# Two-layer hybrid backbone kernel: the second layer's output weights rounded in its half 0 and kept in DRAM, Fourier tables loaded one piece ahead, two splits and one stage put elsewhere in the order

## The chip, the cores and the metric

The kernel runs on one core of a Trainium2 chip. The core has TensorE (PE, matrix products), VectorE (DVE), ScalarE (ACT), GpSimd (POOL) and SyncE (SP), whose queue issues nearly all of this kernel's DMAs, one behind the other; 16 DMA engines carry them. The metric is the time of one execution in device microseconds, less is better. Times below are of single executions taken by the hardware profiler, or medians of timed runs where the text says so.

## The reference

Two layers over 2048 tokens and 256 context tokens of width 1024. A layer normalises, multiplies by one input matrix of 2816 columns, runs three groups of heads, gates them, multiplies by one output matrix, normalises again and adds.

```python
hx = rmsnorm(x, g_pre) * (1 + scale[:, None]) + shift[:, None]
q, k, v, ga, uf, gf, zc, bc, cc, gc = split_cols(hx @ w_in, PROJ_SIZES)
a = window_attention(rope(q), rope(k), v, kc, vc, sink_b)   # 128-token blocks, 256 context keys + 3 blocks
f = fourier_mix(uf, w_fourier)       # 2-D FFT as products with tables, real part, group product
s = short_conv_mix(zc, bc, cc, conv_w, conv_b)
h = concat([a * silu(ga), f * silu(gf), s * silu(gc)])
y = h @ w_out
x_new = x + gate[:, None] * rmsnorm(y, g_post)
```

The first layer also updates the context tokens; the second needs only their keys and values.

## The kernel before

**Precision.** Each fp32 operand is rounded to a high part in fp32r and a low part that holds the rest; a product is three products (hi·hi, hi·lo, lo·hi). The helper `split` makes the two parts: its first letter names the engine of the high part (L79 on DVE, L81 on ACT, L83 on POOL), the second that of the subtraction that gives the low part (L85 on DVE, L87 on POOL).

**Stages.** Each layer has phase 1, in two halves of 1024 tokens (half 0 also takes the context), and phase 2. Phase 1 projects: for each 128-column piece of the input weights (`wr` loaded on SP's queue at L124, split into `wh` and `wl`, two buffers each) `proj` runs eight k-steps of three products, L313, L314 and L315, into `acc`. Behind each k-step `tick()` advances the generators that are registered as fills: modulation, table splits, the FFT stages. In half 1 the fill `ffts` runs the two Fourier transforms: `fft_a`, then `fft_b`, which loads table pieces `ftb` from the DRAM copy `ftd` (L555, three buffers), forms `pf`, splits it into `PQ` and multiplies `PQ` by `AB` into `pm_` (L428 in both). `tab_gen` makes that copy in half 0 of layer 0: a piece `tr` is loaded, split into `th` (ACT and DVE), and stored. `form_b_w` loads the value-and-Fourier weights in four pieces and splits each into `wbh` (DVE) and `wbl`; it runs next to the key weights' piece.

In the profiled execution layer 0 has half 0 until about 345 us, half 1 until about 618 and phase 2 until about 1100; layer 1 half 0 until about 1335, half 1 until about 1604 and phase 2 until the end.

**Phase 2** goes over blocks of 128 tokens, two steps a block (one for each key head). In step s, `u_qk` (A) forms scores `sp` and their exponentials `pt`; `u_pv` (B) transposes them (`tp`), splits them into `ph` and `pl` and multiplies by the values into `op`; `u_out` (C) multiplies by the output weights into `yp` and finishes the block. Strings of letters, one letter a piece, say how the pieces follow each other. In the first steps C's place is taken by three late projections (`late`, through `lt`), and the letters V and W advance `wout_gen`, which makes one half of the output weights each: four loads of 512 KB (`wr<-in_wout`), each split straight into two resident tiles `big`. Phase 2 opens its first loads while phase 1 still runs.

**What sets the order.** The order on an engine is that of the program's text, with a scheduler that places what is ready; `behind(x)` keeps an instruction behind the named one. SP's queue is strictly in order: an issue that waits for a buffer holds everything behind it. `self.last_v` is the DVE instruction of the last split that used DVE; `self.last_st` is the last store of a gate.

```python
                load_wcf()
                wb = self.pool(wbs, f"wb{l}{half}", bufs=1)
                fetch(J_K)
                WB = self.form_b_w(l, wb)
```

Of the kernel before, what the change touches and what calls it, by code (L numbers as in the profile page):

```python
# [8 lines left out]
F32 = mybir.dt.float32  # L9
BF16 = mybir.dt.bfloat16  # L10
F32R = mybir.dt.float32r
# [5 lines left out]
DEPTH = 2  # L17
# [4 lines left out]
KT = 8  # L22
HALF = 1024
CH = 512
# [7 lines left out]
WE_A = ["vv", "av", "vv", "av"]  # L32
WE_B = ["vv", "vp", "vv", "av"]
WV_A = ["vv", "av", "vv", "vv"]
WV_B = ["vv", "av", "vv", "av"]
# [3 lines left out]
ORDER_3A = "bAAWCCBcBCABBAWCBBCBBCcACBCBB"  # L39
ORDER_3B = "bAAWCCBcBCABBAWCBBCBBCcACBCBB"  # L40
# [8 lines left out]
RT = 0.6, 0.594, 0.616, 0.1, 0.15, 0.12, 0.49, 0.16  # L49
# [11 lines left out]
def f(t):  # L61
    return t.bitcast(F32)


class Kern:
# [477 lines left out]
    def fft_b(self, fp, ps, AB, ct):  # L543
# [42 lines left out]
        for _ in range(4):  # L586
            yield
# [24 lines left out]
    def tab_gen(self, p):  # L612
        nc = self.nc
        for k in range(9):
            raw = p.tile([128, 384], F32, name="tr", tag="tr")
            nc.sync.dma_start(raw, self.I["ftab"][:, k])
            yield
            h = p.tile([128, 2, 384], F32R, name="th", tag="th")
            self.split(h[:, 0], h[:, 1], raw, "a", "v")
            nc.sync.dma_start(self.ftd[k], f(h))  # L620
            yield
# [160 lines left out]
    def half(self, l, half, ps, sv, tail):  # L782
# [4 lines left out]
        with ExitStack() as es:  # L787
# [119 lines left out]
            else:  # L907
# [16 lines left out]
                WB = self.form_b_w(l, wb)  # L924
# [47 lines left out]
            if l == 0 and half == 0:  # L972
                mp = self.pool(e3, "mp", bufs=1)
                fills.append(self.start_fill(self.tab_gen(mp), RT[5]))
            for ct in range(2):
# [181 lines left out]
    def u_pv(self, l, p, ps, B, kv):  # L1157
# [28 lines left out]
        for t in range(nkt):  # L1186
            if t + 1 < nkt:
                trans(t + 1)
                yield
            vv = B.vts[t][:, kv * 128:(kv + 1) * 128]  # L1190
            end = t == nkt - 1
            nc.tensor.matmul(op, vv, hl[t][0], start=(t == 0), stop=False)  # L1192
            nc.tensor.matmul(op, vv, hl[t][1], start=False, stop=end)  # L1193
            if kv == 1 and t == 1:
                B.hf = (p.tile([128, 4, 128], F32R, name="hfh", tag="hfh", bufs=1),
                        p.tile([128, 4, 128], F32R, name="hfl", tag="hfl", bufs=1))
                self.split(*B.hf, B.fc, "p", "p")
            yield
# [80 lines left out]

    def wout_gen(self, l, n):  # L1280
        wh, wl = self.big(), self.big()
        self.wout.append((wh, wl))
        for c in range(4):
            with self.behind(self.last_st):
                raw = self.wraw(self.I["wout"][l, n * 4 + c])
            sl = slice(c * 128, (c + 1) * 128)
            with self.behind(self.last_x, self.last_m):
                self.split(wh[:, :, sl], wl[:, :, sl], raw, *((WV_A, WE_A), (WV_B, WE_B))[l][n][c])
            yield
# [23 lines left out]
    def phase2(self, l, ps):  # L1313
# [5 lines left out]
        with ExitStack() as es:  # L1319
# [4 lines left out]
            V, W = self.wout_gen(l, 0), None  # L1324
# [11 lines left out]
            for s in range(nu):  # L1336
# [11 lines left out]
                if s < 4:  # L1348
                    if s == NV:
                        drain(V)  # L1350
                        W = self.wout_gen(l, 1)
                    gens["V"], gens["W"] = V, W
                    emit(gens, (ORDER_0, ORDER_1, ORDER_2, (ORDER_3A, ORDER_3B)[l])[s])
                    if s == 3:
                        drain(W)
                else:
                    emit(gens, ORDER)
# [39 lines left out]
    def run(self):  # L1397
        nc, tc, I = self.nc, self.tc, self.I
        with ExitStack() as es:
# [22 lines left out]
            self.ctx = [I["ctx"], c1]  # L1422
            self.gsl = [dp.tile([128, 2, TOK], F32, name=f"gs_{l}") for l in range(DEPTH)]
# [70 lines left out]
def _layout(x, c, ctx, c_ctx, w_mod, b_mod, g_pre, g_post, w_in, w_out, sink, w_fourier, conv_w, conv_b):  # L1494
# [26 lines left out]
    a["wout"] = ac(wo.reshape(DEPTH, KT, 128, 8, 128).transpose(0, 3, 2, 1, 4)).reshape(DEPTH, 8, 128, KT * 128)  # L1521
    a["sink"] = ac(sink)
# [25 lines left out]
```

## Time and profile before

| | |
|---|---|
| median of 3 runs | 2036.09 us (2033.15 to 2039.77) |
| the profiled execution | 2036.74 us, its span 2034.9 us |
| instructions | 28515 |
| PE busy | 1973.3 us, 97% of the span |
| DVE, ACT, POOL busy | 1242.0, 848.6, 753.6 us |
| TensorE clock granted, mean | 0.989 of full |
| DMA | 291.63 MB, 143 GB/s |

PE is busy nearly throughout, so what PE waits for decides the time; an engine's idle time elsewhere costs nothing by itself. PE's time is lost in two ways: idle gaps, and stretches in which its clock is granted at 1.2 instead of 2.4 GHz, which show as a granted clock below 1.00 in a row for a window. The rows that the prediction uses stand in a section of their own.

### The profile page before, as it was taken

What the parts mean: (1) busy time and instruction counts of PE and PEld (TensorE: products, weight loads), DVE (VectorE), ACT (ScalarE), POOL (GpSimd) and SP (SyncE); (2) the same over time, 40 slices, a digit from 0 to 9 for tenths busy, and PEclk for the clock granted to TensorE, in tenths of its full rate; (3) what the DMA queues carried; (4) which work ended last, traced back from release to release, by engine and by line L of the source; (5) the groups of instructions that cost most, each with busy time, mean ns of one, the idle gap of its engine ahead of it and who ended that gap; (6) DMA issues with size and microseconds to landing.
All of it is one profiled execution on the core that took longest, in us unless ns stands there. A gap on an engine that the chain in (4) does not pass through costs nothing. (4 is left out here: it accounts for less than half of the span.)

```text
span 2034.9 us, 28515 instructions
## 1 busy us (share of the span) xinstructions
PE 1973.3 (97%) x10232; PEld 1670.6 (82%) x10232; DVE 1242.0 (61%) x2239; ACT 848.6 (42%) x1742; POOL 753.6 (37%) x965
## 2 busy tenths in 40 slices
PE   6999999999999999999999999999999999999998
PEld 2898878897887788888877988889788778888886
DVE  7825695646525677777768323142754377777775
ACT  6522212313224556666666322131222356666663
POOL 4322212305342444444455233242234334444442
PEclk8999999999999999999999999999999999999999
DMA  7775654466467344443334533134554834444321
GB/s 298 226 250 158 206 185 141 142 199 186 158 168 218 96 112 115 114 115 104 127 122 137 164 96 94 62 119 132 156 168 141 239 109 116 114 116 113 110 63 42
DMA packets 187038, 291.63 MB, mean 143 GB/s; under 512 B 15608, under 2 KB 119696, under 8 KB 185872
## 3 DMA queue, kind: packets, MB, share of 16 engines
q1 hardware_dynamic: 186896, 289.80, 47.2%
q8 instruction: 81, 1.33, 0.3%
q14 instruction: 61, 0.50, 0.1%
HBM read 214.37 MB, written 75.38 MB: 142 GB/s over the span
## 5 line engine op out<-in xcount | busy, mean ns | idle before, releaser
L315 PE MATMUL acc<-big,wl 128*128 128x512 f32 x1152 | 452.4, 393 | 5.5 <-DVE wl L85 2.9
L313 PE MATMUL acc<-big,wh 128*128 128x512 f32 x1152 | 455.7, 396 | 1.4 <-DVE wh L79 1.4
L314 PE MATMUL acc<-big,wh 128*128 128x512 f32 x1152 | 451.3, 392 | 0.0
L87 POOL TENSOR_TENSOR wl<-wr,wh 128x1024 fp32r<-128x1024 f32 x63 | 162.9, 2586 | 377.4 <-ACT wh L81 234.9
L85 DVE TENSOR_TENSOR pl<-tp,ph 128x512 fp32r<-128x512 f32 x320 | 219.0, 687 | 105.6 <-ACT ph L81 101.2
L1141 ACT ACTIVATE pt<-pt,nm 128x640 f32<-128x640 f32 (+2 forms) x272 | 216.2, 795 | 130.2 <-DVE nm L1138 129.7
L315 PEld LDWEIGHTS acc<-big,wl 128*128 128x128 f32 x1152 | 217.9, 189 | 53.1 <-DVE wl L85 4.2
L313 PEld LDWEIGHTS acc<-big,wh 128*128 128x128 f32 x1152 | 218.5, 190 | 43.8 <-ACT czc L991 1.5
L314 PEld LDWEIGHTS acc<-big,wh 128*128 128x128 f32 x1152 | 218.1, 189 | 42.4 <-DVE big L85 0.2
L81 ACT ACTIVATE ph<-tp 128x512 fp32r<-128x512 f32 x320 | 188.8, 592 | 131.6 <-PE tp L1179 122.1
L1138 DVE CUSTOM_DVE_ANT_0 pt<-sp,mask,nsink 128x640 f32<-128x640 f32 (+2 forms) x256 | 213.3, 841 | 20.7 <-PE sp L1128 15.0
L1153 POOL TENSOR_SCALAR pt<-pt,rv 128x640 f32<-128x640 f32 (+2 forms) x272 | 213.2, 804 | 26.9 <-DVE rv L1151 26.1
L1179 PE MATMUL tp<-ident,pt 128*128 128x128 f32 x1280 | 197.1, 275 | 10.1 <-POOL pt L1153 9.5
L1179 PEld LDWEIGHTS tp<-ident,pt 128*128 128x128 f32 x1280 | 160.1, 141 | 56.8 <-POOL pt L1153 15.3
L358 POOL TENSOR_TENSOR rs<-rs,sinT 128x512 f32<-128x512 f32 x40 | 66.0, 1653 | 170.0 <-DVE rs L356 165.2
L1131 PE MATMUL sp<-kseg,qt 128*128 128x384 f32 (+1 forms) x512 | 128.6, 331 | 0.0
L1228 PE MATMUL yp<-big,hfh 128*128 128x512 f32 x272 | 118.7, 436 | 1.0 <-POOL hfh L83 1.0
L1146 POOL TENSOR_TENSOR es<-nm,nsink 128x4 f32<-128x4 f32 x68 | 14.5, 214 | 283.2 <-DVE nm L1138 283.2
L1228 PE MATMUL yp<-big,hah 128*128 128x512 f32 x272 | 117.1, 431 | 0.1
L1128 PE MATMUL sp<-kctx,qt 128*128 128x256 f32 x544 | 114.2, 292 | 2.9 <-DVE nm L1138 2.0
L1128 PEld LDWEIGHTS sp<-kctx,qt 128*128 128x128 f32 x544 | 95.6, 189 | 16.4 <-DVE nm L1138 3.5
L1230 PE MATMUL yp<-big,hfl 128*128 128x512 f32 x272 | 108.1, 397 | 0.5 <-POOL hfl L87 0.4
(382 smaller groups left out, 3807.9 us busy)
## 6 DMA issues: line engine op xcount, KB each, us to landing
wr<-in_wina SPq DMA_DIRECT2D x76, 512.0 KB, 3.6
qt<-qs SPq DMA_DIRECT2D x34, 512.0 KB, 4.7
wmt<-in_wmodt SPq DMA_DIRECT2D x32, 512.0 KB, 4.3
ftb<-ftd SPq DMA_DIRECT2D x36, 384.0 KB, 3.7
xt<-in_x SPq DMA_DIRECT2D x26, 512.0 KB, 5.8
kseg<-ks SPq DMA_DIRECT2D x24, 512.0 KB, 7.9
xt<-x SPq DMA_DIRECT2D x24, 512.0 KB, 5.1
gat<-gas SPq DMA_DIRECT2D x34, 256.0 KB, 3.1
```

What stands on the lines that cost most here:

```text
L81: nc.scalar.activation(hi, src, AF.Copy, bias=0.0, scale=1.0)
L85: self.last_v = nc.vector.tensor_tensor(lo, src, f(hi), op=ALU.subtract)
L87: nc.gpsimd.tensor_tensor(lo, src, f(hi), op=ALU.subtract)
L313: nc.tensor.matmul(a, wh[:, k, :], hi[:, k, :n], start=(k == 0), stop=False)
L314: nc.tensor.matmul(a, wh[:, k, :], lo[:, k, :n], start=False, stop=False)
L315: nc.tensor.matmul(a, wl[:, k, :], hi[:, k, :n], start=False, stop=(k == KT - 1))
L1128: nc.tensor.matmul(sp[:, 256:512], B.q[:, h, :], self.kctx[:, kv, x, :], start=(x == 0), stop=(x == 1))
L1138: self.last_m = nc.vector.tensor_tensor_reduce(d, x, m, scale=-0.125, scalar=self.nsink[:, h:h + 1], op0=ALU.add, op1=ALU.min, accum_out=n ...
L1141: self.last_x = nc.scalar.activation(pt, pt, AF.Exp, bias=nm[:, hh:hh + 1], scale=-1.0, accum_out=sm[:, hh:hh + 1])
L1153: self.last_p = nc.gpsimd.tensor_scalar(B.pts[kv][g], B.pts[kv][g], rv[:, g:g + 1], 1.0, op0=ALU.mult, op1=ALU.mult)
L1179: nc.tensor.transpose(tp[:, hh * 128:(hh + 1) * 128], pts[hh][:, t * 128:(t + 1) * 128], self.ident)
L1228: nc.tensor.matmul(yp, hh, wh[:, k, :], start=(i == 0), stop=False)
```

## The change

Five edits. (1) The output weights of layer 1 are rounded in half 0 of that layer by a fill, `wout_split`: sixteen pieces of 256 KB are loaded, split on ACT and DVE, and both parts stored in DRAM (`wos`). In phase 2 of layer 1 `wout_load` takes the place of `wout_gen`: sixteen loads of 512 KB straight into the tiles `big`, no split. Layer 1 has strings of its own for the steps 2 and 3. (2) `tab_gen` loads a piece ahead of the one it splits, with two buffers. (3) `form_b_w` stands behind the last DVE split, which is the key weights', in every half but the first. (4) In `fft_b` one yield instead of four stands ahead of the first table products. (5) The split of the Fourier and convolution tile `fct` for the layer's first block comes at that block's last key tile instead of its second.

```diff
-WE_B = ["vv", "vp", "vv", "av"]
-WV_B = ["vv", "av", "vv", "av"]
-ORDER_3A = "bAAWCCBcBCABBAWCBBCBBCcACBCBB"
-ORDER_3B = "bAAWCCBcBCABBAWCBBCBBCcACBCBB"
+ORDER_3 = "bAAWCCBcBCABBAWCBBCBBCcACBCBB"
+ORDER_2B = "bAACACACCCBCBCBCBABBCBBB"
+ORDER_3B = "bWAAWCCBcBCABBAWCBBCBBCcACBWCBB"
-RT = 0.6, 0.594, 0.616, 0.1, 0.15, 0.12, 0.49, 0.16
+RT = 0.6, 0.594, 0.616, 0.1, 0.15, 0.12, 0.49, 0.16, 0.27
...
         h = part(0)
-        for _ in range(4):
-            yield
+        yield
...
+        raw = load(0)
         for k in range(9):
-            raw = p.tile([128, 384], F32, name="tr", tag="tr")
-            nc.sync.dma_start(raw, self.I["ftab"][:, k])
+            yield
+            nx = load(k + 1) if k < 8 else None
             yield
             h = p.tile([128, 2, 384], F32R, name="th", tag="th")
             self.split(h[:, 0], h[:, 1], raw, "a", "v")
             nc.sync.dma_start(self.ftd[k], f(h))
-            yield
+            raw = nx
+        yield
...
                 fetch(J_K)
-                WB = self.form_b_w(l, wb)
+                with self.behind(self.last_v):
+                    WB = self.form_b_w(l, wb)
...
+            elif half == 0:
+                fills.append(self.start_fill(self.wout_split(l, self.pool(e3, "wop", bufs=1)), RT[8]))
...
-            if kv == 1 and t == 1:
+            if kv == 1 and t == (1 if B is not self.Bs[0] else nkt - 1):
...
+    def wout_load(self, l, n):
+        W = [self.big(), self.big()]
+        self.wout.append(W)
+        for c in (2, 3, 0, 1):
+            with self.behind(self.last_st):
+                for t, src in zip(W, self.wos[n]):
+                    self.nc.sync.dma_start(f(t[:, 2 * c:2 * c + 2]), src[:, 2 * c:2 * c + 2])
+            yield
+
+    def wout_split(self, l, p):
...
+        raw = load(0)
+        for i in range(2 * KT):
+            yield
+            nx = load(i + 1) if i + 1 < 2 * KT else None
+            yield
+            h = p.tile([128, 2, CH], F32R, name="wh2", tag="wh2", bufs=2)
+            self.split(h[:, 0], h[:, 1], raw, "a", "v")
+            nc.sync.dma_start(self.wos[i // KT, :, :, i % KT].rearrange("x p c -> p x c"), f(h))
+            raw = nx
+        yield
...
-            V, W = self.wout_gen(l, 0), None
+            wgen = self.wout_load if l else self.wout_gen
+            V, W = wgen(l, 0), None
...
-                    emit(gens, (ORDER_0, ORDER_1, ORDER_2, (ORDER_3A, ORDER_3B)[l])[s])
+                    emit(gens, (ORDER_0, ORDER_1, (ORDER_2, ORDER_2B)[l], (ORDER_3, ORDER_3B)[l])[s])
```

The order on the engines moves as follows at three places. Line numbers of the changed kernel differ: L78 and L84 are the DVE cast and subtraction (L79 and L85 before), L123 the load of a weight piece (L124), L554 that of a table (L555).

DVE in half 1 of layer 0, at the key weights' piece: `wl` is their low part, `wbh` the high part of the four pieces of value weights, `big` and `ht` belong to the tokens' own splits. Before:

```order
L301 SCALAR_TENSOR_TENSOR ht<-xT_3075,G_153,rb_3078 128x512 x2
L79 CAST wbh<-wr 128x768
L303 SCALAR_TENSOR_TENSOR big<-ht,mo_152,big 128x512 x2
L79 CAST wbh<-wr 128x768 x2
L85 TENSOR_TENSOR wl<-wr,wh 128x1024
L79 CAST wbh<-wr 128x768
L79 CAST wh<-wr 128x1024
```

Now:

```order
L300 SCALAR_TENSOR_TENSOR ht<-xT_3075,G_154,rb_3079 128x512 x2
L302 SCALAR_TENSOR_TENSOR big<-ht,mo_153,big 128x512 x2
L84 TENSOR_TENSOR wl<-wr,wh 128x1024
L78 CAST wbh<-wr 128x768 x4
L78 CAST wh<-wr 128x1024
```

Three casts that stood ahead of `wl` now stand behind it.

SP's queue in half 1 of layer 0, at the second pair of table loads of the first `fft_b`: `qs` are stores of the finished queries. Before:

```order
L343 DMA qs_83<-ql 64x512
L124 DMA wr<-in_wina 128x1024
L343 DMA qs_83<-qh 64x512
L343 DMA qs_83<-ql 64x512
L343 DMA qs_83<-qh 64x512
L343 DMA qs_83<-ql 64x512
L555 DMA ftb<-ftd 128x768 x2
```

Now:

```order
L342 DMA qs_84<-ql 64x512
L554 DMA ftb<-ftd 128x768 x2
L123 DMA wr<-in_wina 128x1024
L342 DMA qs_84<-qh 64x512
L342 DMA qs_84<-ql 64x512
L342 DMA qs_84<-qh 64x512
L342 DMA qs_84<-ql 64x512
L554 DMA ftb<-ftd 128x768
```

The pair of table loads moved ahead of one weight load and four stores; layer 1 has the same.

SP's queue at the start of phase 2 of layer 1, behind the last gate stores (`gas<-sg`): `gat` and `fct` are the first block's gates and its Fourier and convolution tile, `lt` the late projections. Before:

```order
L797 DMA gas_10973<-sg 128x512
L124 DMA wr<-in_wout 128x1024 x2
L1164 DMA gat<-gas_10973 128x4x128
L1166 DMA fct<-fs_10974 128x4x128
L124 DMA wr<-in_wout 128x1024
L1166 DMA fct<-fs_10974 128x4x128
L124 DMA wr<-in_wout 128x1024
L1071 DMA gas_10973<-lt 128x512
L1100 DMA qt<-qs_10969 128x8x128
```

Now:

```order
L803 DMA gas_10974<-sg 128x512 x2
L1295 DMA big<-wos 128x1024 x6
L1080 DMA gas_10974<-lt 128x512
L1173 DMA gat<-gas_10974 128x4x128
L1175 DMA fct<-fs_10975 128x4x128
L1295 DMA big<-wos 128x1024 x2
L1109 DMA qt<-qs_10970 128x8x128
L1175 DMA fct<-fs_10975 128x4x128
L1080 DMA gas_10974<-lt 128x512
```

Six loads of 512 KB stand ahead of the first block's `gat` and `fct`, which now also stand behind the first store of `lt`.

## Rows read from the trace of the kernel before

**Rows 1.** The page's first part: busy time of an engine, its share of the span, its instructions.

```profile
PE 1973.3 (97%) x10232; PEld 1670.6 (82%) x10232; DVE 1242.0 (61%) x2239; ACT 848.6 (42%) x1742; POOL 753.6 (37%) x965
```

**Rows 2.** What PE waited for over the whole span: the waiting instruction, the one that released it, then us in total, times, and the longest.

```profile
PE tp L1179 <- POOL pt L1153: 9.5, 15, 1.7
...
PE pf L428 <- DMA ftb<-ftd: 6.1, 2, 3.1
...
PE acc L315 <- DVE wl L85: 2.9, 2, 2.0
PE op L1193 <- DVE pl L85: 2.7, 2, 2.2
PE acc L315 <- POOL wl L87: 2.5, 1, 2.5
...
PE acc L313 <- DVE wh L79: 1.4, 1, 1.4
```

**Rows 3.** Windows of 25 us: length, busy us (and instructions) of PE, PE's weight loads, DVE, ACT and POOL, then PE's granted clock, the busy share of the DMA engines and their GB/s.

```profile
275.00:300.00 25.00, 21.09 (x99) 17.37 (x98) 21.16 (x39) 3.11 (x7) 6.31 (x3) 0.93 0.59 201
...
375.00:400.00 25.00, 22.97 (x95) 18.58 (x94) 10.03 (x12) 4.01 (x7) 11.23 (x6) 0.93 0.44 136
...
475.00:500.00 25.00, 20.66 (x99) 17.02 (x98) 16.09 (x27) 8.41 (x16) 14.12 (x10) 0.93 0.68 186
...
1200.00:1225.00 25.00, 25.00 (x112) 20.68 (x111) 14.06 (x22) 7.28 (x12) 12.00 (x7) 1.00 0.52 126
...
1450.00:1475.00 25.00, 20.83 (x96) 17.14 (x95) 16.73 (x28) 8.68 (x15) 10.32 (x7) 0.93 0.72 199
1600.00:1625.00 25.00, 22.62 (x117) 18.24 (x116) 14.79 (x28) 13.97 (x29) 8.08 (x11) 1.00 0.72 233
1625.00:1650.00 25.00, 22.76 (x117) 18.80 (x117) 21.05 (x34) 11.34 (x25) 9.78 (x11) 0.93 0.51 166
1650.00:1675.00 25.00, 23.14 (x119) 19.01 (x118) 16.90 (x33) 14.64 (x33) 11.77 (x21) 0.93 0.30 72
```

**Rows 4.** DVE in order of time in half 0 of layer 0: start, duration (us), line, operation, in brackets the idle time before it and what ended it.

```profile
288.51 0.56 DVE L85 TENSOR_TENSOR th<-tr,th 128x384 fp32r<-128x384 f32 x1 [1.54 <-ACT th L81]
288.98 1.21 DVE L79 CAST wh<-wr 128x1024 fp32r<-128x1024 f32 x1
290.11 1.21 DVE L195 CUSTOM_DVE_ANT_0 jk<-wmt,sb 128x1024 bf16<-128x1024 f32 x1
...
291.37 3.24 DVE L195 CUSTOM_DVE_ANT_0 jk<-wmt,sb 128x1024 bf16<-128x1024 f32 x1
```

**Rows 5.** POOL at the same place, same columns.

```profile
290.42 3.10 POOL L87 TENSOR_TENSOR wl<-wr,wh 128x1024 fp32r<-128x1024 f32 x1 [0.78 <-DVE wh L79]
```

**Rows 6.** DVE at the key weights in half 1 of layer 0, then PE's gap there (PE's instruction that starts behind it).

```profile
381.55 0.56 DVE L79 CAST wbh<-wr 128x768 fp32r<-128x768 f32 x1 [3.10 <-DMA wr<-in_winb]
387.13 0.56 DVE L79 CAST wbh<-wr 128x768 fp32r<-128x768 f32 x1 [5.03 <-DMA wr<-in_winb]
387.61 1.22 DVE L85 TENSOR_TENSOR wl<-wr,wh 128x1024 fp32r<-128x1024 f32 x1
...
388.88 0.80 PE L315 MATMUL acc<-big,wl 128*128 128x512 f32 x1 [2.03 <-DVE wl L85]
```

**Rows 7.** SP's queue in half 1 of layer 0 at the second pair of table loads, issues in order of time, then two of PE's products there with their waits.

```profile
475.83 0.60 SPq L343 DMA_DIRECT2D qs<-ql  x1
...
483.03 1.02 SPq L555 DMA_DIRECT2D ftb<-ftd  x2
...
480.99 0.50 PE L428 MATMUL pm__4290<-PQ,AB 128*128 128x256 f32 x2 [0.91 <-ACT PQ L81]
...
486.38 0.98 PE L428 MATMUL pf<-ftb,fh 128*128 128x256 f32 x6 [3.09 <-DMA ftb<-ftd]
```

**Rows 8.** DVE over the same stretch.

```profile
476.17 1.75 DVE L357 TENSOR_TENSOR rt<-rt,cosT 128x512 f32<-128x512 f32 x1
...
483.08 0.69 DVE L357 TENSOR_TENSOR rt<-rt,cosT 128x512 f32<-128x512 f32 x1
```

**Rows 9.** The start of phase 2 of layer 1: POOL, DVE, POOL, and two of PE's products with the output weights.

```profile
1613.52 0.62 POOL L83 TENSOR_SCALAR hfh<-fct 128x512 fp32r<-128x512 f32 x1 [3.07 <-DMA fct<-fs]
...
1638.23 2.87 DVE L1070 SCALAR_TENSOR_TENSOR lt<-ht,lt 128x512 f32<-128x512 f32 x1
...
1637.31 3.23 POOL L87 TENSOR_TENSOR big<-wr,big 128x1024 fp32r<-128x1024 f32 x1 [1.29 <-PE tp L1179]
...
1638.43 0.39 PE L1228 MATMUL yp<-big,hfh 128*128 128x512 f32 x1
...
1659.48 0.77 PE L1228 MATMUL yp<-big,hfh 128*128 128x512 f32 x1
```

**Rows 10.** ACT in half 0 of layer 1: the high parts of two weight pieces that follow each other.

```profile
1202.36 1.06 ACT L81 ACTIVATE wh<-wr 128x1024 fp32r<-128x1024 f32 x1 [0.62 <-PE acc L314]
...
1213.54 1.04 ACT L81 ACTIVATE wh<-wr 128x1024 fp32r<-128x1024 f32 x1
```

**Rows 11.** From the page: two groups of splits of 128 x 512 (count, busy us, mean ns of one), and table loads (count, KB, median us from issue to landing).

```profile
L85 DVE TENSOR_TENSOR pl<-tp,ph 128x512 fp32r<-128x512 f32 x320 | 219.0, 687 | 105.6 <-ACT ph L81 101.2
...
L81 ACT ACTIVATE ph<-tp 128x512 fp32r<-128x512 f32 x320 | 188.8, 592 | 131.6 <-PE tp L1179 122.1
...
ftb<-ftd SPq DMA_DIRECT2D x36, 384.0 KB, 3.7
```

More of the change, by code (lines that the diff above doesn't have):

```diff
@@ L613, in tab_gen, with load @@
         nc = self.nc
+        def load(k):
+            t = p.tile([128, 384], F32, name="tr", tag="tr", bufs=2)
+            nc.sync.dma_start(t, self.I["ftab"][:, k])
+            return t
+        raw = load(0)
         for k in range(9):
-            raw = p.tile([128, 384], F32, name="tr", tag="tr")
-            nc.sync.dma_start(raw, self.I["ftab"][:, k])
+            yield
+            nx = load(k + 1) if k < 8 else None
             yield
@@ L1278, in vtile, with load @@
         return self.vtiles[b]
+    def wout_load(self, l, n):
[7 more added lines that the diff above has]
+    def wout_split(self, l, p):
+        nc = self.nc
+        def load(i):
+            t = p.tile([128, CH], F32, name="wo", tag="wo", bufs=2)
+            nc.sync.dma_start(t, self.I["woutk"][l, i // KT, :, i % KT])
+            return t
+        raw = load(0)
[8 more added lines that the diff above has]
+        yield
     def wout_gen(self, l, n):
@@ L1287, in wout_gen @@
             with self.behind(self.last_x, self.last_m):
-                self.split(wh[:, :, sl], wl[:, :, sl], raw, *((WV_A, WE_A), (WV_B, WE_B))[l][n][c])
+                self.split(wh[:, :, sl], wl[:, :, sl], raw, *(WV_A, WE_A)[n][c])
             yield
@@ L1350, in phase2 @@
                         drain(V)
-                        W = self.wout_gen(l, 1)
+                        W = wgen(l, 1)
                     gens["V"], gens["W"] = V, W
-                    emit(gens, (ORDER_0, ORDER_1, ORDER_2, (ORDER_3A, ORDER_3B)[l])[s])
+                    emit(gens, (ORDER_0, ORDER_1, (ORDER_2, ORDER_2B)[l], (ORDER_3, ORDER_3B)[l])[s])
                     if s == 3:
@@ L1422, in run @@
             self.ctx = [I["ctx"], c1]
+            self.wos = dp.tile([2, 2, 128, KT, CH], F32, name="wos")
             self.gsl = [dp.tile([128, 2, TOK], F32, name=f"gs_{l}") for l in range(DEPTH)]
@@ L1521, in _layout @@
     a["wout"] = ac(wo.reshape(DEPTH, KT, 128, 8, 128).transpose(0, 3, 2, 1, 4)).reshape(DEPTH, 8, 128, KT * 128)
+    a["woutk"] = ac(wo.reshape(DEPTH, KT, 128, 2, CH).transpose(0, 3, 2, 1, 4))
     a["sink"] = ac(sink)
```

## The prediction

> **What bounds the kernel now.** I read the page's first part first. PE is busy for 1973.3 of 2034.9 us, and no other engine passes 61% [rows 1], so time is to be had only where PE stands idle, 61.6 us with the program's start and end, or where its clock is down. The waits of PE come next, because they name who is late: many small ones on POOL's normalised scores, which this change doesn't touch, and single long ones on a table load, on low parts of weights and on `pl` [rows 2]. Third, windows of 25 us, because they show both losses in one place. PE is short of 25.00 us by 3.91, 2.03, 4.34 and 4.17 us in the four windows of phase 1 shown, and by 2.38, 2.24 and 1.86 in the three at the start of layer 1's phase 2 [rows 3]. Six of these seven have a granted clock of 0.93: 7% of 25 us, 1.75 us of work not done, so there PE ran for a while at 1.2 GHz after its gap. A gap there costs itself and about 1.75 us more. The rows do not say what size of gap brings this on: 2.03 us did, and 2.38 us, in the window from 1600, which several gaps make up, did not. Between these places PE is at 25.00 of 25 at full clock, as in the window from 1200 [rows 3]; there, work that is added on ACT, DVE or SP costs nothing until it makes PE wait.
>
> The sum is made against the profiled execution, 2036.74 us, which lies 0.65 above the median.
>
> **A, tables loaded ahead.** In half 0 of layer 0 DVE sits idle for 1.54 us in front of `th`, whose high part ACT could not make before the table had landed. Behind `th` (0.56) stands the cast `wh` that PE waits for [rows 4], 1.4 us, and behind that POOL's `wl`, 2.5 us [rows 2]; with 1.75 us of clock the place costs 5.66. The new order has no `th` there, but two of the products with `wmt` that followed the cast now stand ahead of it, at 1.21 us and a 0.08 us read-out each. The cast moves by -1.54 - 0.56 + 2.58: half a microsecond later. Against that, `wl` took 3.10 us beside a DVE product of 3.24 us that took 1.21 without it [rows 4, 5], and its new neighbours are small. I take 1.0 us of gain; -1 if the cast is later and nothing speeds up, 5.7 if the place clears.
>
> **B, value weights behind the key weights.** In half 1 of layer 0 `wl` ended PE's wait at 388.88, a gap of 2.03. It had stood behind a cast at 387.13 that waited for its load, while DVE was free from 382.1 on [rows 6]. With the casts behind it, `wl` runs from there, 1.22 us, and is done at 383.3, ahead of PE's arrival at 386.85. Gap and clock both go: 3.8 us. In layer 1 the same wait is 2.9 - 2.0 = 0.9 us [rows 2]; 0.9. The casts are paced by loads, so they end when they did. Together 4.7; 2.9 if the clock still falls.
>
> **C, three yields fewer in the FFT.** In half 1 PE misses 4.34 us in layer 0 and 4.17 in layer 1, mostly 3.09 for tables and 0.91 for `PQ` [rows 3, 7]; the longest waits for tables are alike in both layers [rows 2]. The tables were issued at 483.03 and used 3.35 us later. In the new order they stand right behind the stores that ended at 476.4 [rows 7], so they are there at 479.8; their buffers are free, since the products that read them are earlier too. But PE also comes earlier. The first products move ahead of five k-steps, three products each at PE's steady 25.00 us for 112 [rows 3]: 15 x 0.223 = 3.4 us. PE then wants `PQ` at about 480.1 - 3.4 = 476.7 (480.1 is where the gap of 0.91 began that ended at 480.99 [rows 7]). DVE is held until 477.9 by a 1.75 us product [rows 8], then needs 0.69 for the low part of `PQ` [rows 11]: 478.6. So about 1.9 us of idle time moves from the tables to `PQ`, and the tables, wanted about 1.3 us after that, are just in time. The idle time falls by 2.4. With the clock kept that is 4.2 of gain, without it 2.4; I take 3.3 a layer, 6.6 in all, bounds 4.8 and 11.5 (all gaps and both clock losses gone).
>
> **D, no splits at the start of phase 2.** Eight splits of 128 x 1024 leave: on DVE, ACT and POOL. PE misses 6.48 us in the three windows, and 3.5 by the clock in two of them [rows 3]. The waits are on what stood behind those splits: `pl` behind a subtraction beside which `lt` took 2.87 us and POOL's subtraction 3.23 [rows 9], and the exponential sums behind POOL's wait of 3.07 for `fct` [rows 9], which edit 5 takes away. I keep about 1.5 us idle and half a clock loss: 7.5 us of gain, bounds 4 and 10. The cover is that the loads come in time. Six loads go out when the gate stores have gone, right behind half 1's end at 1604: 3.15 MB at the 233 GB/s of that window [rows 3] is 13.5 us, so about 1619 with the stores, against a first use at 1638.43. Of the second half's eight, four are issued behind the second block's `gat`, which waits until the first block's gating is done, somewhere between the two products shown, 21 us apart [rows 9]: 2.1 MB, 9 us, so little may be left; but the quarters used first are loaded first. Without cover, a wait of a few us.
>
> **E, splits added in half 0 of layer 1.** Sixteen on ACT at 0.592 us, sixteen on DVE at 0.687 [rows 11], 4.2 MB read and 8.4 MB written, each store on SP's queue. ACT is busy for 7.28 and DVE for 14.06 of 25 us in the window shown, DMA engines half [rows 3]: 0. Weight pieces follow each other 11.2 us apart and take 1.06 on ACT [rows 10] and up to 3.10 on POOL [rows 5], so some 7 us of delay is covered.
>
> **F, waits that I can't place.** The queues are re-ordered from the FFT to the first blocks, and every gap so far cost between 0.9 and 5.9 us. I put 2 us against the sum (0 to 6).
>
> Sum: 1.0 + 4.7 + 6.6 + 7.5 + 0 - 2 = 17.8, 2018.9 on the profiled execution, **2018.5** with half of the 0.65 taken off.
>
> A rule that speaks against E: the Trainium skill (GPSIMD Engine Reference, section Specifications) says that GpSimd shares its SBUF interfaces with VectorE and contends with DVE instructions that have two SBUF inputs. The trace agrees: the same product takes 1.75 and 0.69 us [rows 8], the longer one beside work on POOL. All sixteen new subtractions are of this kind; by the rule each could grow by some 1.06 us, 17 us over DVE, still within its idle time; the sum stays, and the same rule helps D.
>
> **The rivals.**
> *The gaps shrink, the clock still falls.* PE keeps gaps of one to two us in B, C and D, and each brings its clock loss. For it speaks that 2.03 us was enough [rows 3]; against it that B's gap should vanish altogether. Four losses that I count as gone come back, 7 us: **2025.5**.
> *The loads of the output weights come late.* SP's queue is in order, and each load of a phase that used to be spread between splits now stands in a bunch ahead of `gat`, `fct`, `qt` and `lt`. D gives back its 7.5, or that and a wait of 3 with its clock loss: **2026 to 2031**. Against it speak the 19 us between landing and use in the first half.
> *No change.* The waits moved are replaced by their neighbours' (C's `PQ` in place of the tables, A's products in place of `th`, a late `fct`): **2033 to 2038**. That the edits don't take effect is excluded by the orders shown.
> *Slower: weights late in half 0 of layer 1.* A `wos` store waits on SP for its DVE half, and the weight load behind it waits too. The decisive point is the 7 us of E: beyond it each microsecond costs one at each of about nine pieces in which the new splits run. At 3 us over, that is 27 on top of the forecast: **2046**. Against it: DVE and ACT have idle time there, and the new pieces are paced by k-steps.
>
> **How the numbers follow.** Chances: forecast (2010 to 2024) 0.55, clock rival 0.17, late loads 0.12, no change 0.09, slower 0.07. A change under 0.3%, 6.1 us, is what a measurement can't tell from none. Faster: 0.55 + 0.17 + 0.11 = 0.83; same: 0.09 + 0.01 = 0.10; slower 0.07. The range of 2010 to 2031 holds nearly all of the forecast and the next two. Its low end is A, C and D near their bounds.
>
> **What would show it.** B: no wait of L315 for DVE's `wl` in half 1. C: no PE wait for `ftb` of 3 us; instead one of under 2 us for `PQ`. D: no `big` on DVE after 1604, windows above 24 us busy there, no wait for a `wos` load. E: PE still at 25.00 from 1175 to 1335. A: the windows at 275 to 300 little changed. The prediction is wrong if PE waits for `big<-wos`, for `wh` or `wl` in half 0 of layer 1, or if the clock rows still show 0.93 at 375 and after 1625.

## The result and the profile after

The changed kernel takes 2020.51 us (median of 4 runs, 2014.01 to 2022.1) against 2035.25 for the kernel before in the same runs (median of 4, 2033.15 to 2039.77). The ratio is 0.9913, with a 95% interval of 0.9898 to 0.9928: 17.7 us saved, 14.7 to 20.8; the two medians by themselves lie 14.7 apart. The profiled execution took 2020.18 us with a span of 2018.4, against 2036.74 and 2034.9: 16.5 us.

Busy time of an engine, its share of the span, instructions (against [rows 1]):

```profile
PE 1966.3 (97%) x10232; PEld 1668.6 (83%) x10232; DVE 1243.4 (62%) x2243; ACT 854.8 (42%) x1755; POOL 737.0 (37%) x964
```

PE's work is the same 10232 products. Its busy time fell by 7.0 us, at least in part because fewer products ran at 1.2 GHz (mean granted clock 0.991 against 0.989), and its idle time inside the span (2034.9 - 1973.3 before, 2018.4 - 1966.3 now) by 9.5. The view of what PE waited for says which idle time that is (us in total, times, longest; against [rows 2]):

```profile
PE tp L1188 <- POOL pt L1162: 6.9, 11, 1.9
...
PE pf L427 <- DVE fh L84: 3.8, 3, 2.1
PE pf L427 <- DMA ftb<-ftd: 3.6, 2, 2.2
PE acc L314 <- POOL wl L86: 1.8, 1, 1.8
...
PE pm__4276 L427 <- DVE PQ L84: 1.4, 1, 1.4
PE accb L410 <- DVE ql L84: 1.1, 1, 1.1
...
PE pm__13846 L427 <- DVE PQ L84: 0.9, 1, 0.9
...
PE acc L312 <- DVE mo L189: 0.9, 1, 0.9
```

The waits for DVE's `wl` and for `pl` at the start of phase 2 are gone. The longest table wait fell from 3.1 to 2.2. New are waits for `fh`, the low part of the transform's own data; those for `PQ` on DVE grew from 0.34 us to 1.4 and 0.9; a new `accb` wait for `ql` stands in layer 1. No wait names a `wos` load.

The windows (length, busy us of PE, its weight loads, DVE, ACT, POOL, granted clock, DMA share, GB/s; against [rows 3]):

```profile
275.00:300.00 25.00, 22.29 (x104) 18.39 (x104) 19.30 (x35) 2.19 (x5) 6.41 (x3) 0.93 0.51 188
375.00:400.00 25.00, 25.00 (x117) 21.38 (x116) 7.77 (x11) 2.83 (x5) 11.55 (x6) 1.00 0.45 140
450.00:475.00 25.00, 22.93 (x99) 18.93 (x98) 20.43 (x53) 6.60 (x11) 10.04 (x5) 0.93 0.49 136
475.00:500.00 25.00, 22.71 (x125) 19.54 (x124) 20.16 (x31) 9.00 (x19) 15.07 (x12) 1.00 0.77 218
550.00:575.00 25.00, 22.81 (x118) 19.57 (x117) 9.67 (x14) 5.90 (x12) 11.91 (x9) 0.93 0.30 105
1200.00:1225.00 25.00, 25.00 (x112) 20.70 (x111) 15.01 (x23) 8.74 (x14) 11.01 (x6) 1.00 0.61 180
1450.00:1475.00 25.00, 23.18 (x116) 19.74 (x115) 17.97 (x28) 9.80 (x18) 15.12 (x10) 0.93 0.82 224
1600.00:1625.00 25.00, 25.00 (x138) 21.20 (x138) 13.51 (x34) 16.30 (x38) 9.08 (x17) 1.00 0.83 273
1625.00:1650.00 25.00, 25.00 (x142) 21.30 (x141) 18.06 (x35) 14.94 (x32) 7.97 (x12) 1.00 0.88 261
1650.00:1675.00 25.00, 25.00 (x142) 21.44 (x142) 19.10 (x38) 15.34 (x36) 10.82 (x21) 1.00 0.46 124
```

Three things are to be seen. The windows from 1600 are full. So is that from 375, whose clock loss is gone. But the windows from 450 and from 550, at 25.00 and 24.81 before, now lack 2.07 and 2.19 us, both with a clock of 0.93: new losses in layer 0's transforms.

Where in the program the 16.5 us were won shows when the starts of the same product are set side by side:

| PE's product | before | after | difference |
|---|---|---|---|
| value projection, half 1 of layer 0 | 401.00 | 396.06 | -4.9 |
| a projection between the two transforms, half 1 of layer 0 | 527.37 | 522.46 | -4.9 |
| first scores, phase 2 of layer 0 | 619.73 | 618.40 | -1.3 |
| first scores, phase 2 of layer 1 | 1604.03 | 1598.59 | -5.4 |
| end of the span | 2034.9 | 2018.4 | -16.5 |

PE gained 4.9 us by the value projection of layer 0, still had them between the two transforms, and lost 3.6 of them in the second one. Phase 2 of layer 1 alone brought 11.1.

### The profile page after: what moved, and what is told of

Same layout as the page of the kernel before. It is cut to its first block, busy times and chain, and to the rows that moved or that the text cites. A ratio compares the mean times of both kernels' runs of the same rounds, so it can differ in the third digit from the quotient of the medians.

```text
span 2018.4 us, 28589 instructions
## 1 busy us (share of the span) xinstructions
PE 1966.3 (97%) x10232; PEld 1668.6 (83%) x10232; DVE 1243.4 (62%) x2243; ACT 854.8 (42%) x1755; POOL 737.0 (37%) x964
## 5 line engine op out<-in xcount | busy, mean ns | idle before, releaser
L86 POOL TENSOR_TENSOR wl<-wr,wh 128x1024 fp32r<-128x1024 f32 x63 | 157.5, 2500 | 382.6 <-ACT wh L80 260.7
L84 DVE TENSOR_TENSOR pl<-tp,ph 128x512 fp32r<-128x512 f32 x320 | 219.2, 687 | 110.9 <-ACT ph L80 106.3
L1147 DVE CUSTOM_DVE_ANT_0 pt<-sp,mask,nsink 128x640 f32<-128x640 f32 (+2 forms) x256 | 213.2, 841 | 17.7 <-PE sp L1137 13.8
L1162 POOL TENSOR_SCALAR pt<-pt,rv 128x640 f32<-128x640 f32 (+2 forms) x272 | 208.7, 786 | 24.2 <-DVE rv L1160 23.0
L1237 PE MATMUL yp<-big,hfh 128*128 128x512 f32 x272 | 118.9, 437 | 1.0 <-POOL hfh L82 1.0
L1238 PE MATMUL yp<-big,hfh 128*128 128x512 f32 x272 | 107.8, 396 | 0.0
```

The lines of the kernel that those rows point to most:

```text
L84: self.last_v = nc.vector.tensor_tensor(lo, src, f(hi), op=ALU.subtract)
L1147: self.last_m = nc.vector.tensor_tensor_reduce(d, x, m, scale=-0.125, scalar=self.nsink[:, h:h + 1], op0=ALU.add, op1=ALU.min, accum_out=n ...
L1162: self.last_p = nc.gpsimd.tensor_scalar(B.pts[kv][g], B.pts[kv][g], rv[:, g:g + 1], 1.0, op0=ALU.mult, op1=ALU.mult)
L1237: nc.tensor.matmul(yp, hh, wh[:, k, :], start=(i == 0), stop=False)
```

## The experiments

The expectations were written as the work went on, and each says what it calls theory and rival. The first theory was read off the trace of the changed kernel: each edit alone does what its stretch shows there, with a gain for edits 1 and 5 and for edit 3 and a loss for edit 4; its rival, that edit 4 earns the 6.6 of the prediction. Both fell on edits 3 and 4. What took their place: in half 1 of layer 0 PE does not set the time behind the value projection, so a lead won ahead of it (edit 3) is waited off in the first transform as long as that has four yields, and what edits 3 and 4 do depends on each other.

**Single edits on the kernel before.** Their diffs are those of the change.

Edits 1 and 5 alone:

> The kernel before with edits 1 and 5 alone (output weights of layer 1 rounded in half 0 and kept in DRAM; the first block's fct split at its last key tile). Theory: all 6.5 us of idle and both clock stretches at the start of layer 1's phase 2 go, and the splits added in half 0 cost nothing: 10 to 11 us less, 0.5%. Rival: part of the gain seen with all edits came from the other edits (earlier gate stores), and this alone gives 7 us or less, or PE waits in half 0 of layer 1.

Measured: 2027.43 us, ratio 0.9949 (0.9932 to 0.9967), 10.4 us saved. Its windows at the start of phase 2 of layer 1:

```profile
1600.00:1625.00 25.00, 24.74 (x133) 20.83 (x132) 10.63 (x25) 12.69 (x28) 8.12 (x14) 1.00 0.85 284
1625.00:1650.00 25.00, 25.00 (x138) 21.18 (x137) 17.46 (x36) 15.64 (x34) 7.08 (x12) 1.00 0.74 247
1650.00:1675.00 25.00, 25.00 (x142) 21.50 (x142) 19.29 (x37) 15.22 (x34) 10.84 (x21) 1.00 0.75 181
```

The 6.48 us of idle time are gone but for 0.26, and both clock losses with them. From the first scores of layer 1 to the end of the span, the four profiled kernels without edit 1 take 429.8 to 431.4 us, the ten with it 419.8 to 420.6. The term D is thus about 10.5, and it adds to whatever stands ahead of it.

Edit 2 alone:

> The kernel before with edit 2 alone (Fourier tables loaded a piece ahead in half 0 of layer 0). Theory of step A: the place at 289 to 294 us goes from 3.9 us idle to between 2.5 and 3, the clock still falls: about 1 us less, too little for the timing to show. Rival: the place clears, 5.7 us less.

Measured: 2036.94, ratio 0.9995 (0.9981 to 1.0009). PE waits 0.99 and 1.81 at the place instead of 1.37 and 2.54 [rows 2], and the window still shows 0.93: about a microsecond, too little for the timing.

Edit 3 alone:

> The kernel before with edit 3 alone (the value weights' casts behind the key weights' split). Theory of the prediction's step B: the gap at 388.9 us of layer 0 goes with its stretch at the lower clock, and the 0.91 us gap at 1375 us goes: 3.7 + 0.9, about 4.6 us less, 0.23%. Rival (gaps only move): the late value weights make a new wait of one to two us, so the gain is under 2 us and a wait of PE for wbh or wbl appears.

Measured: 2039.51, ratio 1.0013 (1.0000 to 1.0026): no gain, rather a loss. The wait for `wl` at 388.88 is gone, but a hundred microseconds on so is the lead that this had brought. Two of PE's products in layer 0's first transform, and one in half 0 of layer 1, in brackets the wait and who ended it; then the window around the first two:

```profile
481.89 2.06 PE L428 MATMUL pm__4290<-PQ,AB 128*128 128x256 f32 x6 [4.43 <-ACT PQ L81]
487.43 1.65 PE L428 MATMUL pf<-ftb,fh 128*128 128x256 f32 x6 [2.19 <-DMA ftb<-ftd]
...
1145.99 0.69 PE L411 MATMUL accb<-wbh,big 128*128 128x384 f32 x1 [2.88 <-DVE ql L85]
```

```profile
475.00:500.00 25.00, 18.33 (x77) 15.19 (x77) 14.94 (x26) 9.01 (x16) 12.13 (x8) 0.73 0.66 180
```

The wait for `PQ` grew from 0.91 to 4.43, and the granted clock of that window fell to 0.73. In half 0 of layer 1, of which the prediction said nothing for this edit, the casts behind the key weights delay `ql`; with a stretch at the lower clock, PE falls 4.2 us further behind there.

Edit 4 alone:

> The kernel before with edit 4 alone (one yield instead of four ahead of the FFT's table products). Theory drawn from the two traces: the two table waits of 3.1 us go, but waits for fh, PQ and a later table take their place; about 3 us slower, with PE waits for fh of about 2 us and for ftb of about 2 us in half 1 of layer 0. Rival, the prediction's step C: 6.6 us faster, with a PQ wait of under 2 us as the only one left.

Measured: 2035.8, ratio 0.999 (0.9976 to 1.0003): about 2 us of gain, if any, so neither a loss nor 6.6. In layer 0 waits of 1.57 (`PQ`), 0.88 (`fh`) and, in the second transform, 1.84 (tables) stand in place of 0.91 and 0.34 (`PQ`) and 3.09 (tables), all three in the first transform; layer 1 has 0.98, 0.88 and 2.12. The starts of the same products tell the two transforms apart (the last column is the change):

| PE's product | before | edit 4 alone | the change |
|---|---|---|---|
| value projection, half 1 of layer 0 | 401.00 | 400.56 | 396.06 |
| a projection between its transforms | 527.37 | 523.17 | 522.46 |
| first scores, phase 2 of layer 0 | 619.73 | 618.79 | 618.40 |
| value projection, half 1 of layer 1 | 1385.68 | 1384.14 | 1381.60 |
| a projection between its transforms | 1517.13 | 1511.45 | 1510.43 |
| first scores, phase 2 of layer 1 | 1604.03 | 1601.89 | 1598.59 |

Alone, the edit wins 3.8 us in the first transform of layer 0 and 4.1 in that of layer 1, and loses 3.3 and 3.5 in the second ones.

The four ratios make 10.4 + 1.0 - 2.6 + 2.0 = 10.8 us; the whole change brought 17.7 in the first comparison and, timed again below, 14.9. Each ratio is uncertain by some 3 us, and by the medians the four make 11.7 and the whole 14.7 and 15.9, so the difference of 3 to 7 is only a hint that edits earn together what they don't alone; it is followed up below.

**The changed kernel again, and edit 4 undone in it.**

> The changed kernel once more, as the measure for the runs beside it: about 0.991 of the kernel before, 15 to 18 us less.

Measured: 2021.01, ratio 0.9927 (0.9908 to 0.9946). The program is the same, the clock is not (two windows of this profile, to be set beside those of the first):

```profile
275.00:300.00 25.00, 21.85 (x107) 18.09 (x107) 19.36 (x37) 1.93 (x4) 6.61 (x3) 1.00 0.52 189
1450.00:1475.00 25.00, 22.73 (x120) 19.30 (x119) 19.40 (x31) 10.11 (x18) 15.19 (x11) 1.00 0.84 244
```

Here 3.15 and 2.27 us of idle time went by at full clock, where 2.71 and 1.82 had brought 0.93. In the first transform of layer 0 the loss did not go, it moved: the window from 450 is at 1.00 now and that from 475 at 0.93.

Edit 4 undone:

```diff
         h = part(0)
-        yield
+        for _ in range(4):
+            yield
```

> The changed kernel with edit 4 undone (four yields again). Theory: edit 4 costs about 3 us net (new waits for fh, PQ and ftb with their clock stretches, against the two table waits it removes), so this is about 3 us faster than the changed kernel, and its trace shows the two table waits of 3.1 us and no wait for fh. Rival, step C of the prediction: 6.6 us slower than the changed kernel.

Measured: 2023.28, ratio 0.9936 (0.9916 to 0.9956), 2.3 us above the changed kernel timed beside it; the two intervals overlap. The wait for `PQ` is back at its full size, and a table wait behind it:

```profile
480.37 0.50 PE L427 MATMUL pm__4291<-PQ,AB 128*128 128x256 f32 x2 [4.66 <-ACT PQ L80]
...
485.78 1.65 PE L427 MATMUL pf<-ftb,fh 128*128 128x256 f32 x6 [2.07 <-DMA ftb<-ftd]
```

So edit 4 is worth about 2 us with the others as without them: neither the loss that I had read off the changed kernel's trace nor the 6.6 of the prediction; what it wins in the first transforms it mostly gives back in the second ones.

**What the tables wait for: the loads on another queue.** The kernel with four yields, its table loads issued by ACT:

```diff
-                nc.sync.dma_start(f(tabs[k]), self.ftd[k])
+                nc.scalar.dma_start(f(tabs[k]), self.ftd[k])
```

> The changed kernel with four yields and the table loads of both transforms issued on ScalarE's queue instead of SyncE's. If the table waits of 3.1 us come from the stores and the weight load that stand ahead on SyncE's queue, they shrink to under 1 us, the clock stays up, and this is 8 to 9 us faster than the one with four yields. Rival: the tables are late because their buffers are released late, whatever queue issues them; then the waits stay at about 3 us.

Measured: 2019.96, ratio 0.9915 (0.9901 to 0.993), 3.3 below the kernel with four yields, by intervals that overlap, and well short of the 8 to 9 expected. All waits for `ftb` are gone; that for `PQ` in layer 0 stays, and layer 1 has one of 1.86 now:

```profile
481.62 2.06 PE L427 MATMUL pm__4291<-PQ,AB 128*128 128x256 f32 x6 [4.65 <-ACT PQ L80]
```

The tables were late because of what stood ahead of them on SP's queue. That is a second cause beside the one for `PQ`; taken away by itself, it leaves PE to wait for `PQ`.

**One yield in the first transform of a half only.** In the second one the new order puts two table loads behind the store of the convolution, as DVE, SP and PE of the changed kernel show:

```profile
552.10 3.42 DVE L384 TENSOR_TENSOR cy<-cy,cbm 128x1025 f32<-128x1025 f32 x1 [2.29 <-POOL cbm L366]
```

```profile
555.55 0.32 SPq L385 DMA_DIRECT2D fs<-cy  x1
555.97 1.50 SPq L554 DMA_DIRECT2D ftb<-ftd  x2
```

```profile
561.82 0.97 PE L427 MATMUL pf<-ftb,fh 128*128 128x256 f32 x6 [2.19 <-DMA ftb<-ftd]
```

The store can go out only when DVE has made `cy`, and the table loads stand behind it in SP's order. Hence the edit:

```diff
         h = part(0)
-        yield
+        for _ in range(4 if ct else 1):
+            yield
```

> The changed kernel with one yield in the first Fourier transform of a half and four in the second. Theory: the table waits of the second transform (2.2 us with a clock stretch in layer 0, 1.4 us in layer 1) come from the three yields fewer there and go, about 5 us faster than the changed kernel. Rival: they come from the first transform's lead of three k-steps, which shifts the second as well; then they stay or move, and the time is within 2 us of the changed kernel.

Measured: 2014.23, ratio 0.9887 (0.9871 to 0.9904): 23 us faster than before and 6.8 below the changed kernel timed beside it. This version beats both kernels. The windows of the second transforms are full now, in layer 0 (from 550) and layer 1 (from 1525):

```profile
550.00:575.00 25.00, 25.00 (x135) 21.50 (x134) 9.32 (x18) 6.06 (x13) 10.96 (x11) 1.00 0.41 132
...
1525.00:1550.00 25.00, 25.00 (x141) 21.73 (x140) 9.48 (x18) 7.07 (x15) 12.55 (x11) 1.00 0.39 127
```

**Is the first transform bound by its own input?** The transform starts on DVE when `fx`, one load of both halves' tokens, has landed. To have it earlier, layer 0's first transform reads half 0's tokens twice, in two loads of half the size, in the kernel with four yields; half 1's tokens are left out of that transform.

```diff
-        nc.sync.dma_start(x, self.us[:, 2:18, ct * 128:(ct + 1) * 128])
+        if ct == 0 and not getattr(self, "fx_done", False):
+            self.fx_done = True
+            for i in (0, 8):
+                nc.sync.dma_start(x[:, i:i + 8], self.us[:, 2:10, :128])
+        else:
+            nc.sync.dma_start(x, self.us[:, 2:18, ct * 128:(ct + 1) * 128])
```

> The changed kernel with four yields; the first Fourier transform of layer 0 reads half 0's tokens twice, in two loads, instead of all sixteen blocks in one (half 1's tokens are left out of that transform), so its input no longer waits for half 1's last stores. Theory: PE's wait of 4.7 us for PQ in half 1 of layer 0 is the end of a chain on DVE and ACT that starts when the transform's input lands at 446 us, whatever PE gained before; with the input about 5 us earlier the wait falls below 1.5 us, and the execution is 3 to 5 us shorter than the one with four yields. Rival: PQ is late because of the query chunks ahead of it on ACT and POOL; then the wait stays above 3.5 us.

Measured: 2019.2, ratio 0.9909 (0.9884 to 0.9934), against 0.9936 for four yields, timed in other runs: the 3 to 5 us expected fit, but the intervals overlap. DVE's first operation on `fx` and PE's two products:

```profile
440.75 1.23 DVE L451 TENSOR_TENSOR fa<-fx 128x1024 f32<-128x1024 f32 x1 [6.45 <-DMA fx<-us]
```

```profile
476.22 0.73 PE L427 MATMUL pm__4292<-PQ,AB 128*128 128x256 f32 x4 [0.25 <-DVE PQ L84]
...
481.42 1.34 PE L427 MATMUL pf<-ftb,fh 128*128 128x256 f32 x6 [3.76 <-DMA ftb<-ftd]
```

With the input 5.3 us earlier the wait of 4.66 for `PQ` is down to 0.25. What PE wants next is the tables, still late by their queue. That the time of `PQ` follows the input, and not PE, is plain from this table of starts, too (PE at the value projection; DVE's first operation on `fx`; DVE's low part of the first `fh` and of the first `PQ`, half 1 of layer 0):

| kernel | PE | `fx` | `fh` | `PQ` | `PQ` - `fx` |
|---|---|---|---|---|---|
| before | 401.00 | 446.65 | 466.38 | 481.10 | 34.45 |
| edit 3 alone | 398.39 | 447.60 | 467.34 | 482.00 | 34.40 |
| edit 4 undone | 396.33 | 446.08 | 465.82 | 480.47 | 34.39 |
| edit 4 alone | 400.56 | 446.13 | 465.86 | 477.32 | 31.19 |
| the change | 396.06 | 445.45 | 465.20 | 476.61 | 31.16 |
| one yield in the first transform only | 395.57 | 444.84 | 464.56 | 475.98 | 31.14 |
| the same without edit 3 | 399.38 | 448.80 | 468.52 | 479.91 | 31.11 |
| edit 4 undone, input early | 396.66 | 440.75 | 456.43 | 475.49 | 34.74 |

PE's arrival differs by 5.4 us, and the way from `fx` to `PQ` is 34.4 to 34.7 us with four yields and 31.1 to 31.2 with one, wherever PE is. `fh` follows `fx` after 19.7 in every row but the last, where it takes 15.7 and `PQ` still moves by 5.0 only: behind `fh` a piece of the queries stands ahead of `PQ`. ACT with four yields:

```profile
479.20 0.63 ACT L80 ACTIVATE qh<-rt 128x512 fp32r<-128x512 f32 x1 [4.40 <-DVE rt L358]
479.74 0.58 ACT L80 ACTIVATE PQ<-pf 128x512 fp32r<-128x512 f32 x1
```

`qh` is the high part of that piece, `rt` its rotation, which goes to and fro between DVE and POOL behind the transform's own work on DVE. With one yield ACT makes `PQ` at 474.04, ahead of the piece; that is where the 3.3 us between the two groups of rows come from. So the rival of this run holds in part: the query pieces are a stretch of the way, and the input sets when the way begins.

**Edit 3 and edit 5 in the better version and in the change.** Edit 3 left out of the version above:

```diff
-                with self.behind(self.last_v):
-                    WB = self.form_b_w(l, wb)
+                WB = self.form_b_w(l, wb)
```

> The kernel with one yield in the first transform and four in the second, without edit 3. Theory: in layer 0 the gap at 387 us comes back (2 us) and the waits of PE at the first transform for fh and PQ shrink by as much, since the transform's input doesn't move: the same time there within a clock stretch. In layer 1 a gap of 0.7 to 1 us comes back. So 0 to 3 us slower. Rival: edit 3's gain holds in full, 4.6 us slower or more.

Measured: 2020.13, ratio 0.9917 (0.9892 to 0.9941), about 6 us slower than with it, each against its own before, and 5.0 slower than the version with edit 3 in half 1 only, timed beside it below, whose runs all lie below these. Here, with one yield, edit 3 earns about what the prediction gave it, if not by the way that it gave; the 0 to 3 expected for this run were too little. The wait for `wl` is back at 388.81 (2.18), and one in the transform besides:

```profile
478.02 0.50 PE L427 MATMUL pm__4276<-PQ,AB 128*128 128x256 f32 x2 [0.58 <-ACT PQ L80]
...
480.64 0.74 PE L427 MATMUL pm__4276<-PQ,AB 128*128 128x256 f32 x4 [2.12 <-DVE PQ L84]
```

`fx` landed later here than in any other kernel, at 448.80; why is not settled, since its load waits on SP behind stores whose data come late for several reasons. In this profile the loss passes through `PQ`: it starts 3.9 us later, as `fx` does by 4.0, and a stretch at the lower clock behind it adds 1.5. Whether `fx` was late because PE came late by the wait for `wl` stays open; edit 4 alone has that wait as well, and its `fx` started at 446.13.

Edit 3 in half 1 only:

```diff
-                with self.behind(self.last_v):
+                with self.behind(self.last_v if half else None):
```

> The kernel with one yield in the first transform and four in the second, with edit 3 in the two halves 1 only. In half 0 of layer 1, edit 3 makes PE wait 1.1 to 2.9 us for ql at the value projection in place of a wait of 1.1 us for the token splits. Theory: without it there the first wait goes and the second comes back: 0 to 1 us less, 5 less where the clock had fallen. Rival: no difference in the trace there.

Measured: 2015.09, ratio 0.9893 (0.9865 to 0.9921). The `accb` wait for `ql` in half 0 of layer 1 goes, a wait of 1.08 for `ht` at 1108.35 comes back, and the time is the same.

Edit 5 undone in the change:

```diff
-            if kv == 1 and t == (1 if B is not self.Bs[0] else nkt - 1):
+            if kv == 1 and t == 1:
```

> The changed kernel with edit 5 undone (the first block's fct split at its second key tile again). Theory: POOL's exponential sums wait behind that split for fct, which now lands later than before, behind six loads; PE waits for nm at the start of layer 1's phase 2, 1.5 us or more and up to 6, so 2 to 8 us slower than the changed kernel. Rival: the wait came from the splits on DVE alone; then no wait of PE above 0.5 us appears there and the time is the changed kernel's.

Measured: 2020.45, ratio 0.992 (0.9893 to 0.9947): no difference from the change. POOL in that kernel:

```profile
1612.42 2.70 POOL L1162 TENSOR_SCALAR pt<-pt,rv 128x512 f32<-128x512 f32 x4 [0.31 <-DVE rv L1160]
1615.55 0.62 POOL L82 TENSOR_SCALAR hfh<-fct 128x512 fp32r<-128x512 f32 x1 [0.43 <-POOL pt L1162]
```

The split `hfh` stands behind two groups of `pt` either way, and `fct` has landed by then. The wait of 3.07 [rows 9] went with edit 1's new order, not with edit 5.

## Why the prediction was right, and where it was not

The forecast of 2018.5 lies 2 us under the median. Its sum for the profiled execution was 17.8 against 16.5 measured, but terms missed in both directions, and C's by more than the whole of it.

**A** (1.0 predicted). PE was 0.75 ahead behind this place, and the window shows the clock loss still, as said. The cast `wh` started at 289.35, where the prediction had it half a microsecond later than 288.98 [rows 4]. What shortened was its length, 1.21 to 0.68, and POOL's `wl`, 3.10 [rows 5] to 2.38.

**B** (4.7: 3.8 and 0.9). Right at the place: PE's lead grows from 0.75 to 4.9 by the value projection, and the window from 375 is full; in layer 1 it grows by 1.2 at the same place. Wrong in layer 0 as a term of a sum: the step took it that a lead at 390 is kept. With four yields it runs into the stage of the table above, whose time is set by `fx` and by the work behind it on DVE, POOL and ACT. Edit 3 alone is 2.6 ahead of before at the value projection and 2.2 behind it between the transforms, edit 4 undone 4.7 ahead and 0.3 behind. In the change the 4.9 are still there between the transforms, because edit 4 makes this stage shorter.

**C** (6.6) is the step that failed. It worked out the wait for `PQ` from before's own times: DVE done at 478.6, 1.9 us idle. In the run the low part was done at 477.3 and PE waited 1.41, and the tables were in time, as predicted; all the signs that it named for C came true: they asked for no table wait of 3 us and a `PQ` wait under 2, not for new waits elsewhere. Three things are missing in it:

```profile
466.87 1.56 PE L427 MATMUL pf<-ftb,fh 128*128 128x256 f32 x7 [2.08 <-DVE fh L84]
477.35 0.74 PE L427 MATMUL pm__4276<-PQ,AB 128*128 128x256 f32 x4 [1.41 <-DVE PQ L84]
479.20 1.46 PE L427 MATMUL pf<-ftb,fh 128*128 128x256 f32 x10 [0.88 <-DVE fh L84]
```

The first table products need `fh` too, and moved ahead of five k-steps they meet its split, 2.08 us, since B had brought PE there earlier; edit 4 alone does not show this wait. The second `fh` costs 0.88. And, the largest, the generator runs twice a half: the second transform's loads moved behind a store, 2.19 us and a clock loss. That makes 6.56 us of idle time in layer 0, where 4.34 had been, with two clock losses for one. In layer 1 waits of 0.94, 0.89 and 1.44 stand for 0.77, 0.34 and 3.06. By the starts in the table at edit 4 alone, the change wins nothing in layer 0's first transform and 2.6 us in layer 1's, and loses 3.6 and 1.3 in the second ones: -2.3 in place of +6.6, with what B's lead lost in it. At the first transforms the step was right for the edit alone, 3.8 and 4.1 where it put 3.3 each; the second ones, of which it said nothing, take most of that. Undone by itself, the edit is worth 2. The bounds of 4.8 to 11.5 took in neither.

**D** (7.5, bounds 4 to 10) was mis-sized: 11.1 in this execution, 10.5 over all kernels. I had kept 1.5 us of idle time and half a clock loss, but 6.48 and both losses, 3.5, went: 9.98. Another microsecond I can't place. The reason given for the exponential sums, edit 5, was wrong; `pl`, the other one, agrees with the rows. The cover held:

```profile
1599.88 4.03 SPq L1295 DMA_DIRECT2D big<-wos  x6
...
1633.97 2.05 SPq L1295 DMA_DIRECT2D big<-wos  x4
```

```profile
big<-wos SPq DMA_DIRECT2D x16, 512.0 KB, 6.4
```

Six loads go out at once, as forecast, and the last four wait behind the second block's `gat`. They land 6.4 us after their issue (median), and no product waits for them. The rival of late loads has no sign in the trace.

**E** (0) held: PE is at 25.00 in the window from 1200, with DVE at 15.01 and ACT at 8.74 us, and the rival of late weights shows nothing.

**F** (-2): no wait outside C's stretches used it up. In half 0 of layer 1 one wait of 1.1 was exchanged for another, and from the first scores of layer 0, where PE was 1.3 ahead, to the key weights of layer 1, where it was 2.9 ahead, 1.6 us were gained that no term had.

**The clock rival** (7 us back) came true in part: the windows from 450, 550 and 1450 still show 0.93. But the premise that each gap costs 1.75 us more holds for one execution at a time. The same single wait of 2.54 us for `wl` stands in a window at 0.93 in one kernel (edit 4 alone) and, with a wait of 0.92 ahead of it, at 1.00 in another (edits 1 and 5):

```profile
275.00:300.00 25.00, 22.39 (x105) 18.43 (x104) 22.12 (x41) 3.14 (x7) 6.78 (x3) 0.93 0.63 211
```

```profile
275.00:300.00 25.00, 21.55 (x106) 17.83 (x105) 21.30 (x37) 3.13 (x7) 6.32 (x3) 1.00 0.58 199
```

I count such a gap better as itself plus a loss that comes in some executions. At 1.75 us a place that could account for much of the spread of 2014 to 2022, whose ends had a mean granted clock of 0.994 and 0.990; this was not tested.

In sum: the direction was right because of D, which has one cause, a run of its own and a gain clear of noise. The size was near in part by luck. C fell 8.9 us short of its term, 4.9 of them in the second transforms, which it had left out, and 4.0 in the first ones, where B's lead met the stage's own time; D gave 3.6 more than its term and B 0.7, and where F had set 2 aside, 1.6 were gained.

## What to carry to other kernels

A wait that is removed is a lead, not yet a gain: follow the lead to the next place where another engine's chain sets the time, here some 90 us on, and ask there how far PE may come early. Edits that lie on one such way are priced together, with the arrival that the other edit brings, and a generator that runs at several places is priced at each: a sign that looks at one of them can come true while the gain goes at the other. On an in-order queue, look at what a moved load now stands behind: a store that waits for its data stops every load after it.

## What the runs showed of the hardware

- The granted clock after a gap isn't the same from one execution to the next: the changed kernel's window from 275 was at 0.93 with 2.71 us idle and at 1.00 with 3.15, that from 1450 at 0.93 with 1.82 and at 1.00 with 2.27.
- In the kernel before, DVE's casts of 128x1024, with one input, took 0.68 or 0.69 us where POOL was idle. Three that started while a POOL instruction was running took 1.11 to 1.21 (one of them in [rows 4]) and ended 0.54 or 0.55 us after it; a fourth, started 0.12 us before POOL's end, took 0.69. Two that started 0.16 and 0.48 us ahead of one took 0.69. Two that started just ahead, by 0.06 and 0.01 us, took 0.68 and 0.72, and POOL's instruction then took 0.97 or 0.98 us, where another of its kind took 0.48. So what counts there is which of the two starts first, and the later one is held. The two products of [rows 8] fit this: both had POOL's work beside them, the one of 0.69 us started 0.11 ahead of it, and the one of 1.75 ended 0.54 after POOL's instruction. The product of 1.21 us in [rows 4], too, had started 0.31 ahead of POOL's `wl`, which the prediction took for absent. The prediction had looked for this only where an instruction has two inputs. The Trainium skill (GPSIMD Engine Reference, section Specifications) names a second kind that contends, DVE instructions in a 2-port mode; the cast's times agree with it, though no row shows the mode.
- Moving loads from SP's to ACT's queue took away table waits of 2.07 and 3.13 us, with 384 KB a load as before and 3.9 us from issue to landing against 3.8 (medians): the time had been spent ahead of the issue, not in the transfer.
